# A decoder block on one core: the two halves of a two-bank PSUM tile used two blocks apart, a third pair of row buffers in the last phase, and late tiles opened two blocks sooner

## The chip, the core and the metric

The kernel runs on one core of a Trainium2 chip. The metric is the device time of one execution in microseconds (us). Three runs of the kernel before gave 1812.57, 1811.48 and 1809.37 us, so the median is 1811.48 us. A fourth run was profiled. All rows in this document are from profiles of that kind.

The engines have short names here. PE is the matrix engine, PEld its weight load. DVE is the vector engine, ACT the scalar engine, POOL the GpSimd engine and SP the engine that issues most transfers. SBUF is the on-chip working memory. PSUM is the accumulator memory that matmuls write to, in eight banks.

## The reference

One decoder layer runs over 512 tokens of width 1024, in fp32. It has two mixing branches (gated linear attention, and sliding-window attention with sinks), then a PEER layer: each token picks 128 of 16384 single-neuron experts and adds their outputs.

```python
h = rmsnorm(x); proj = h @ w_in                        # all head groups and gates
y_a = gla(...) @ w_branch_a;  y_b = swa(...) @ w_branch_b
x = x + (sigmoid(gate_a) * y_a + sigmoid(gate_b) * y_b) @ w_out
xn = rmsnorm(x)                                        # PEER from here
scores = per head, two halves of the query against 128 sub-keys each
idx, gate = top 16 of the 16 x 16 sums, softmax        # 8 heads x 16 = 128 experts a token
hid = gelu(einsum('lkd,ld->lk', expert_u[idx], xn))
x = x + einsum('lk,lkd->ld', gate * hid, expert_v[idx])
```

## The kernel before

The first 668 us hold the mixing branches and the scores. All that is changed lies behind, in the PEER layer, which the kernel computes in two ways at once.

**Dense part, 360 tokens.** All 16384 experts are taken in 128 blocks of 128. For block b, `h_step(b)` forms the first products (inputs times U rows, 24 matmuls of 360 columns into one PSUM bank, name `hp`), and ACT takes their gelu (line 1367) into an SBUF ring. Later `v_step(b)` multiplies the gelu by the gates (`w_a`, `w_b`) and adds it, against the V rows, into eight output banks. The blocks are done in three phases (`PHASES`, line 77): first products of blocks 0 to 91, second products of 0 to 91, first products of 92 to 111, second products of 92 to 111, first products of 112 to 127, second products of 112 to 127. The text calls these H0, V0, H1, V1, H2 and V2. Each 512 KB weight block is loaded by SP (`raw`), rounded by ACT (`whi`, line 149), and its rest is formed by DVE (`wlo`, line 159).

**Sparse part, 152 tokens.** The other tokens gather the U and V rows of their own experts. There are 154 slots of 1 MB (`gather`, line 1264). POOL issues a gather (line 1285). DVE does a product with the token (line 1300), ACT a gelu and a gate (lines 1258 and 1259), DVE an addition (line 1317). While H0 runs, a slot has a single buffer (`row`, two of them, in a pool `R`). From `late[0]` on, slots come in pairs (`rows`, tag `gbuf`, two buffers of 2 MB). `issue(k)` runs at the end of the addition of slot k-1 and requests all slots below a horizon of k + 2, and of k + 3 when late.

**What else lies in H0.** Scores become expert numbers and gates; the gates of the 360 dense tokens are built block by block with small matmuls (`gp`, line 1165), copied by ACT (`gbuild`, also tag `gbuf`) and written to memory (`gd`); one token group's gates go out by 128 scatters on POOL (line 1120). V0 reads them back as `gt` tiles (`g_load`, line 1382). The first two `g_load`s are issued on POOL at block `N0 - GL`; the tiles lie in a pool `Lt` that takes the memory of `R`, so the last early slot must be added up first (`while early[0]: step()`, at block `N0 - TAIL - 1`).

**Order.** Each engine runs its instructions in the order in which the program writes them. Where steps of the sparse part go between blocks is decided while the program is built: `pump` keeps running sums of the cost of PE, DVE, POOL and DMA work, and takes a step when the others are not ahead of PE.

**Banks of the first products.** In H0 blocks with b % 4 of 0 and 1 write the two halves of one two-bank tile (`hp2`, tag `S2`), blocks with b % 4 of 2 and 3 write single banks `M0` and `M1` (lines 1352 to 1357). The other banks are in use by `gp` and the transposes.

**The end.** The last two blocks of V2 are done column block by column block (c from 7 down to 0, line 1568). Each gets 6 matmuls, an addition on DVE (`yT`, line 1483), three transposes on PE (`yt`) two column blocks later, two additions into the output tile (`xr`, lines 1492 and 1493), and two steps of the sparse part. What is left of the sparse part comes behind (`flush`), then a last small product (`xo`) folds its sum in.

Of the kernel before, what the change touches and what calls it, by code (L numbers as in the profile page):

```python
# [47 lines left out]
NOO = 4  # L48
AHEAD = 3
LEAD = 23  # L50
TAIL = 3
SLACK = 3.0
DUTY = 0.97
LAND = 10.0
POOLQ = 9.0
GL = 4

HD = (3, 2, 2, 3, 2, 2, 2, 0, 0)
XG = 24
# [22 lines left out]
def tile_block(ctx, tc, xT, wst, smalls, wgk2, keysT, uT, vv, uv_rows, out):  # L82
# [1161 lines left out]
            yield  # L1244

    late, early, used, acc2 = [False], [0], [-1], []
    nxt, born, end = [], {}, [False]
    sel = XP.tile([128, XG], F32, name="sel")
    nc.gpsimd.tensor_tensor(sel, ident[:, 0:XG], ident[:, XG:2 * XG], OP.add)
    for r in range(2, XR):  # L1250
# [13 lines left out]
    def gather():  # L1264
# [7 lines left out]

        def issue(k):
            nonlocal grp, n
            while n < min(n_, k + (3 if late[0] else 2)):
                for i in range(min(2 if late[0] else 1, n_ - n)):
                    if late[0]:
                        if i == 0:
                            grp = Dn.tile([128, 2, 2 * D], F32, name="rows", tag="gbuf", bufs=2)
                        rows[n] = grp[:, i]  # L1280
                    else:
                        rows[n] = R.tile([128, 2 * D], F32, name="row", tag="er", bufs=2)
                        early[0] = n + 1
                    ix = use[slots[n][0]][3]
                    nc.gpsimd.indirect_dma_start(  # L1285
                        out=rows[n], out_offset=None, in_=uv_rows,
                        in_offset=bass.IndirectOffsetOnAxis(ap=ix[:, slots[n][1]:slots[n][1] + 1], axis=0))
                    n += 1
                    pool[0] += 1.5
                    born[n - 1] = max(pe[0], pool[0])  # L1290
                    xfer(2.54)
# [57 lines left out]

    def h_step(b, each=None):  # L1350
        w = get("U", b)
        if b < N0 and b % 4 < 2:
            if b % 2 == 0:
                two[0] = PS.tile([128, 2, 512], F32, name="hp2", tag="S2")
            bank = two[0][:, b % 2]
        else:
            bank = PS.tile([128, 512], F32, name="hp", tag=f"M{b % 2}")
        ps = proj(w, XN, n=TD, c0=TG, bank=bank, each=each)
        p = b // 2
        spill = NRP <= p < N0 // 2  # L1360
# [142 lines left out]
    for ph, (b0, b1) in enumerate(PHASES):  # L1503
# [38 lines left out]
        for c, tg in enumerate(BANKS):  # L1542
            accs[c] = big[:, c] if c < 2 else PS.tile([128, 512], F32, name="oa", tag=tg)
        last = b1 == NB
        for b in range(b0, b1 - 2 if last else b1):
            p = b // 2
            if not ph and b % 2 == 0 and p:
# [8 lines left out]
            v_step(b, b == b0, b == b1 - 1)  # L1556
            pump()
            if b == NB - 6:
                end[0] = True
                xr = P.tile([128, 4, D], F32, name="xr", tag="hhi")  # L1560
                nc.sync.dma_start(xr[0:TB, 1], x1s[XG:, 1])
                nc.sync.dma_start(xr[0:XG, 0], x1s[0:XG, 1])
# [95 lines left out]
```

## Time and profile before

| | us |
|---|---|
| median of three runs | 1811.48 |
| profiled execution, its own time | 1812.18 |
| its span, first to last instruction | 1810.4 |
| PE busy | 1727.5 (95%) |
| DVE busy | 1320.8 (73%) |
| ACT busy | 766.0 (42%) |
| POOL busy | 753.7 (42%) |
| PE idle for gelu in H0 (line 1367) | 16.9 |

The profiled execution lies 0.7 us above the median, and 1.8 us of it lie outside the span. PE is busy nearly all the time, so each microsecond in which PE stands still, or runs at the lower of its two clock levels (the profile gives the granted clock as a share of 2.4 GHz), is a candidate for a loss. A row of a timeline tells in brackets how long the engine stood idle before the instruction, and which instruction ended that. DMA share is the mean busy share of the core's 16 transfer engines.

### The profile page before, as it was taken

What the parts mean: (1) busy time and instruction counts of PE and PEld (TensorE: products, weight loads), DVE (VectorE), ACT (ScalarE), POOL (GpSimd) and SP (SyncE); (2) the same over time, 40 slices, a digit from 0 to 9 for tenths busy, and PEclk for the clock granted to TensorE, in tenths of its full rate; (3) what the DMA queues carried; (4) which work ended last, traced back from release to release, by engine and by line L of the source; (5) the groups of instructions that cost most, each with busy time, mean ns of one, the idle gap of its engine ahead of it and who ended that gap; (6) DMA issues with size and microseconds to landing.
All of it is one profiled execution on the core that took longest, in us unless ns stands there. A gap on an engine that the chain in (4) does not pass through costs nothing.

```text
span 1810.4 us, 26362 instructions
## 1 busy us (share of the span) xinstructions
PE 1727.5 (95%) x9828; PEld 1588.5 (88%) x9828; DVE 1320.8 (73%) x2547; ACT 766.0 (42%) x1350; POOL 753.7 (42%) x472
## 2 busy tenths in 40 slices
PE   7899999999997999999999999999999999999995
PEld 5676688987885889999999999999999999999993
DVE  7647714346246996987767745888988999898896
ACT  5445523335244234355455543444444444443441
POOL 3333444444544451677777671212222233233231
PEclk9999999999998999999999999999999999999996
DMA  4223542222243233589899898999999999999994
GB/s 159 77 70 94 149 133 81 70 82 73 91 143 132 77 108 135 137 254 258 263 275 276 246 296 314 392 400 400 396 401 405 379 379 394 355 393 350 402 346 175
DMA packets 164837, 432.68 MB, mean 239 GB/s; under 512 B 34789, under 2 KB 80229, under 8 KB 144613
## 3 DMA queue, kind: packets, MB, share of 16 engines
q1 hardware_dynamic: 118597, 254.69, 39.8%
q0 software_dynamic: 40928, 163.04, 25.5%
q10 hardware_dynamic: 5184, 13.27, 1.9%
q8 instruction: 77, 1.26, 0.3%
q14 instruction: 51, 0.42, 0.1%
HBM read 389.30 MB, written 41.62 MB: 238 GB/s over the span
## 4 chain that ended last, share of the span: by engine, by line
PE 78%; DVE 9%; DMA 5%; ACT 4%; issue 2%; POOL 1%; SPq 0%; POOLq 0%; DVEq 0%; ACTq 0%
PE hp L210 25%; PE oa L1419 19%; PE mm L210 17%; PE oacc L1419 6%; PE mm L227 4%; DMA rows<-in_uv_rows_dram,misc 4%; PE gp L1165 3%; PE sc L954 1%; DMA gt<-g 1%; DVE accy L1317 0%; DVE stt L434 0%; ACT hw L1367 0%; DMA xt<-in_xT_dram 0%; DVE stt L435 0%; DMA qb<-in_keysT_dram 0%
## 5 line engine op out<-in xcount | busy, mean ns | idle before, releaser
L149 ACT CAST whi<-raw 128x1024 fp32r<-128x1024 f32 x349 | 363.2, 1045 | 112.8 <-DMA raw<-in_vv_dram 22.5
L1285 POOL DMA_INDIRECT rows<-in_uv_rows_dram,misc x130 | 185.9, 1430 | 516.3 <-DVE accv L1317 405.6
L159 DVE TENSOR_TENSOR wlo<-raw,whi 128x1024 fp32r<-128x1024 f32 x250 | 306.0, 1224 | 103.2 <-issue 46.3
L210 PE MATMUL hp<-xh,whi 128*128 128x360 f32 x1024 | 344.3, 336 | 20.9 <-ACT hw L1367 13.4
L159 POOL TENSOR_TENSOR wlo<-raw,whi 128x1024 fp32r<-128x1024 f32 x99 | 245.0, 2478 | 242.8 <-ACT whi L149 230.0
L210 PE MATMUL hp<-xl,whi 128*128 128x360 f32 x1024 | 337.2, 329 | 0.0
L210 PE MATMUL hp<-xh,wlo 128*128 128x360 f32 x1024 | 336.3, 328 | 0.0
L1120 POOL DMA_INDIRECT g<-w,addr x128 | 229.9, 1796 | 90.0 <-issue 42.4
L1419 PE MATMUL oa<-wh,wlo 128*128 128x360 f32 x768 | 252.6, 329 | 1.0 <-DVE wlo L159 1.0
L1419 PE MATMUL oa<-wh,whi 128*128 128x360 f32 x768 | 252.9, 329 | 0.0
L1419 PE MATMUL oa<-wl,whi 128*128 128x360 f32 x768 | 252.1, 328 | 0.0
L210 PEld LDWEIGHTS hp<-xh,whi 128*128 128x128 f32 x1024 | 193.9, 189 | 28.0 <-ACT hw L1367 18.5
L210 PEld LDWEIGHTS hp<-xl,whi 128*128 128x128 f32 x1024 | 193.8, 189 | 0.0
L210 PEld LDWEIGHTS hp<-xh,wlo 128*128 128x128 f32 x1024 | 193.5, 189 | 0.0
L1419 PEld LDWEIGHTS oa<-wh,wlo 128*128 128x128 f32 x768 | 145.5, 189 | 1.3 <-DVE wlo L159 1.3
L1419 PEld LDWEIGHTS oa<-wl,whi 128*128 128x128 f32 x768 | 145.6, 190 | 0.0
L1419 PEld LDWEIGHTS oa<-wh,whi 128*128 128x128 f32 x768 | 145.6, 190 | 0.0
L1317 DVE SCALAR_TENSOR_TENSOR accv<-rows,misc,accv 128x1024 f32<-128x1024 f32 x104 | 133.5, 1284 | 11.8 <-ACT misc L1259 11.8
L1300 DVE SCALAR_TENSOR_TENSOR rows<-rows,xtok 128x1024 f32<-128x1024 f32 x104 | 127.1, 1222 | 5.5 <-DMA rows<-in_uv_rows_dram,misc 5.0
L1258 ACT ACTIVATE misc<-misc 128x1 f32<-128x1 f32 (+1 forms) x154 | 31.5, 204 | 221.7 <-DVE rows L1300 221.7
L210 PE MATMUL mm<-hhi,whi 128*128 128x512 f32 x264 | 107.1, 406 | 0.9 <-DVE gb L610 0.9
L210 PE MATMUL mm<-hhi,wlo 128*128 128x512 f32 x264 | 103.1, 391 | 0.0
(583 smaller groups left out, 3318.8 us busy)
## 6 DMA issues: line engine op xcount, KB each, us to landing
raw<-in_uT_dram SPq DMA_DIRECT2D x128, 512.0 KB, 5.5
raw<-in_vv_dram SPq DMA_DIRECT2D x128, 512.0 KB, 8.6
raw<-in_wst_dram SPq DMA_DIRECT2D x93, 512.0 KB, 3.5
gd<-gbuild SPq DMA_DIRECT2D x56, 256.0 KB, 6.0
gt<-gd SPq DMA_DIRECT2D x30, 464.0 KB, 10.6
hs<-hw ACTq DMA_DIRECT2D x36, 360.0 KB, 7.0
ring<-hs SPq DMA_DIRECT2D x36, 360.0 KB
g<-zero SPq DMA_DIRECT2D x16, 512.0 KB, 5.7
```

The source lines that it names most:

```text
L149: nc.scalar.copy(hi, self.raw[u])
L159: self.lo_eng(u).tensor_tensor(lo, r, hi.bitcast(F32), OP.subtract)
L210: nc.tensor.matmul(ps[:, :n], a[:, kb, :], b[:, kb, c0:c0 + n], start=(kb == 0 and i == 0), stop=(kb == KB - 1 and i == 2))
L227: nc.tensor.matmul(banks[t], a[:, kb, t * 128:(t + 1) * 128], b[:, k, :], start=(first and k == 0 and i == 0), stop=(last and k == kk - 1 ...
L954: nc.tensor.matmul(sc[:, t], qp[:, t * 128:(t + 1) * 128], ky[hp], start=True, stop=True)
L1120: i = nc.gpsimd.indirect_dma_start(out=g3, out_offset=bass.IndirectOffsetOnAxis(ap=addr[:, c:c + 1], axis=0), in_=w3[:, c:c + 1], in_offse ...
L1165: nc.tensor.matmul(p[:, k], o[:, 0, k], o[:, 1, k], start=True, stop=True)
L1258: nc.scalar.activation(h, h, AF.Gelu)
L1285: nc.gpsimd.indirect_dma_start(out=rows[n], out_offset=None, in_=uv_rows, in_offset=bass.IndirectOffsetOnAxis(ap=ix[:, slots[n][1]:slots[n ...
L1300: nc.vector.scalar_tensor_tensor(cur, cur, 1.0, xs_[kind][0:m, :], OP.mult, OP.mult, accum_out=hc)
L1317: nc.vector.scalar_tensor_tensor(a_, cur, h_[0:m, s_:s_ + 1], a_, OP.mult, OP.add)
L1419: nc.tensor.matmul(accs[c][:, 0:TD], v_[:, cs], a, start=(first and i == 0), stop=(last and i == 2))
```

## The change

Four edits. The halves of `hp2` now go to blocks with b % 4 of 0 and 2, and the blocks between them use `M0` and `M1` in turn. `GL` and `TAIL` each grow by 2, so that the first `g_load`s, the switch to pairs and the close of pool `R` come two blocks sooner (blocks 86, 83 and 86 in place of 88, 85 and 88), and the gate building is spread over 58 blocks in place of 60. In V2 a third pair buffer is used: the memory of the tag `hlo`, which held the low part of the inputs until the last first product. `end[0]` is set at the start of V2 in place of block 122, and while it holds, the horizon grows by 2; two products may run ahead of the additions, as they did from block 122 on before.

```diff
-TAIL = 3
+TAIL = 5
-GL = 4
+GL = 6
...
-            while n < min(n_, k + (3 if late[0] else 2)):
+            while n < min(n_, k + (3 if late[0] else 2) + 2 * end[0]):
...
-                            grp = Dn.tile([128, 2, 2 * D], F32, name="rows", tag="gbuf", bufs=2)
+                            pool_, tag, k_ = (P, "hlo", 1) if end[0] and en[0] % 3 == 0 else (Dn, "gbuf", 2)
+                            en[0] += end[0]
+                            grp = pool_.tile([128, 2, 2 * D], F32, name="rows", tag=tag, bufs=k_)
...
-        if b < N0 and b % 4 < 2:
-            if b % 2 == 0:
+        if b < N0 and b % 2 == 0:
+            if b % 4 == 0:
                 two[0] = PS.tile([128, 2, 512], F32, name="hp2", tag="S2")
-            bank = two[0][:, b % 2]
+            bank = two[0][:, b % 4 // 2]
         else:
-            bank = PS.tile([128, 512], F32, name="hp", tag=f"M{b % 2}")
+            bank = PS.tile([128, 512], F32, name="hp", tag=f"M{(b // 2 if b < N0 else b) % 2}")
...
         last = b1 == NB
+        end[0] = last
...
             if b == NB - 6:
-                end[0] = True
```

On PE, in H0, the first matmuls of blocks 8 to 13 stand like this before, with the semaphore that each waits for. `whi101` is the weight of block 8, and each next number is the next block; `hp2` is the two-bank tile, `hp` a single bank.

```order
L210 MATMUL hp2_5775<-xh_4270,whi101_5664 128x360 [waits Activation_49]
...
L210 MATMUL hp2_5775<-xh_4270,whi102_5695 128x360 [waits Activation_49]
...
L210 MATMUL hp_5843<-xh_4270,whi103_5728 128x360
...
L210 MATMUL hp_5880<-xh_4270,whi104_5771 128x360
...
L210 MATMUL hp2_5914<-xh_4270,whi105_5808 128x360 [waits Activation_49]
...
L210 MATMUL hp2_5914<-xh_4270,whi106_5839 128x360 [waits Activation_49]
```

The same six first matmuls on PE now:

```order
L210 MATMUL hp2_5775<-xh_4270,whi101_5664 128x360 [waits Activation_49]
...
L210 MATMUL hp_5812<-xh_4270,whi102_5696 128x360
...
L210 MATMUL hp2_5775<-xh_4270,whi103_5728 128x360 [waits Activation_49]
...
L210 MATMUL hp_5880<-xh_4270,whi104_5771 128x360
...
L210 MATMUL hp2_5914<-xh_4270,whi105_5808 128x360 [waits Activation_49]
...
L210 MATMUL hp_5953<-xh_4270,whi106_5840 128x360
```

The wait for ACT at the second half stood one block after the first half, and stands two blocks after it now; the wait of the next tile stood three blocks after the second half and stands two after it now.

On DVE, at the end, the work behind the `wlo` of the last weight block stands like this before. `accy` is an addition of the sparse part, `rows` with `misc` a product, `yT` and `xr` belong to the output columns.

```order
L159 TENSOR_TENSOR wlo_16062<-raw_15996,whi_16026 128x1024
L1317 SCALAR_TENSOR_TENSOR accy<-rows,misc,accy 120x1024
L1300 SCALAR_TENSOR_TENSOR rows,misc<-rows,xtk_14474 120x1024
L1483 TENSOR_TENSOR yT<-yT,oa 128x360
...
L1300 SCALAR_TENSOR_TENSOR rows,misc<-rows,xtk_14474 120x1024
L1483 TENSOR_TENSOR yT<-yT,oa 128x360
L1492 TENSOR_TENSOR xr<-xr,yt 104x128
L1493 TENSOR_TENSOR xr<-xr,yt 128x2x128
L1317 SCALAR_TENSOR_TENSOR accy<-rows,misc,accy 120x1024 x2
L1483 TENSOR_TENSOR yT<-yT,oacc 128x360
```

The same place on DVE now:

```order
L159 TENSOR_TENSOR wlo_16077<-raw_16010,whi_16041 128x1024
L1319 SCALAR_TENSOR_TENSOR accy<-rows,misc,accy 120x1024
L1302 SCALAR_TENSOR_TENSOR rows,misc<-rows,xtk_14370 120x1024
L1485 TENSOR_TENSOR yT<-yT,oa 128x360
...
L1302 SCALAR_TENSOR_TENSOR rows,misc<-rows,xtk_14370 120x1024
L1485 TENSOR_TENSOR yT<-yT,oa 128x360
L1494 TENSOR_TENSOR xr<-xr,yt 104x128
L1495 TENSOR_TENSOR xr<-xr,yt 128x2x128
L1319 SCALAR_TENSOR_TENSOR accy<-rows,misc,accy 120x1024 x2
L1485 TENSOR_TENSOR yT<-yT,oa 128x360
```

Behind that `wlo` stand 8 additions and 6 products before, and 6 additions and 4 products now. Before, the last two additions are followed by the seventh of the eight `yT`; now by the fifth. Counted from the start, two slots more are done at each of these points: 26 in place of 24 at the end of H0, 148 in place of 146 additions at the last `wlo`. Line numbers behind the edits are higher by 2.

## Rows read from the trace of the kernel before

**Rows 1.** Waits of PE, whole span: who, for whom, us, times, longest.

```profile
PE hp L210 <- ACT hw L1367: 13.4, 18, 1.8
...
PE hp L210 <- ACT ev L1473: 4.0, 1, 4.0
...
PE hp L210 <- ACT ring L1367: 3.5, 5, 1.2
```

**Rows 2.** The chain that ended last, merged: start, length, what, matmuls.

```profile
1065.50 16.21 PE hp L210 x96
1082.25 16.20 PE hp L210 x96
...
1481.04 59.70 PE hp L210 x360
```

**Rows 3.** Timeline of PE, in H0 and at the start of V0: start, length.

```profile
921.52 0.43 PE L210 MATMUL hp<-xh,whi 128*128 128x360 f32 x1 [1.80 <-ACT hw L1367]
...
922.65 0.50 PE L210 MATMUL hp<-xh,whi 128*128 128x360 f32 x1
922.95 0.50 PE L210 MATMUL hp<-xl,whi 128*128 128x360 f32 x1
...
925.65 0.48 PE L210 MATMUL hp<-xl,whi 128*128 128x360 f32 x1
...
1113.88 0.67 PE L1419 MATMUL oacc<-wh,whi 128*128 128x360 f32 x1 [2.70 <-ACT wh L1403]
...
1114.83 0.67 PE L1419 MATMUL oacc<-wl,whi 128*128 128x360 f32 x1 [0.27 <-DVE wl L1409]
...
1120.39 0.40 PE L1419 MATMUL oa<-wl,whi 128*128 128x360 f32 x1
```

**Rows 4.** Timeline of ACT, late in H0.

```profile
1093.38 1.05 ACT L149 CAST whi<-raw 128x1024 fp32r<-128x1024 f32 x1 [6.36 <-DMA hs<-hw]
1094.33 0.46 ACT L1367 ACTIVATE hw<-hp 128x360 f32<-128x360 f32 x1
```

**Rows 5.** Timeline of POOL, late in H0.

```profile
1094.84 1.64 POOL L1285 DMA_INDIRECT rows<-in_uv_rows_dram,misc  x1 [12.54 <-DMA raw<-in_uT_dram]
...
1101.36 0.59 POOL L1384 DMA_DIRECT2D gt<-gd  x1 [3.19 <-DVE accv L1317]
```

**Rows 6.** Timeline of DVE, from H0 into V0.

```profile
1099.40 1.28 DVE L1317 SCALAR_TENSOR_TENSOR accv<-row,misc,accv 128x1024 f32<-128x1024 f32 x1 [0.90 <-ACT misc L1259]
...
1112.52 0.44 DVE L1398 TENSOR_TENSOR wr<-ring,gt 128x272 f32<-128x272 f32 x1 [0.78 <-DMA gt<-g]
```

**Rows 7.** Stretches: length, busy PE, PEld, DVE, ACT, POOL, granted clock, DMA share, GB/s.

```profile
780.00:1110.00 330.00, 317.38 (x2025) 312.79 (x2024) 224.94 (x402) 159.98 (x234) 230.30 (x137) 0.99 0.92 276
960.00:990.00 30.00, 28.88 (x186) 28.28 (x185) 21.61 (x40) 15.43 (x24) 22.23 (x14) 1.00 0.97 277
1742.00:1752.00 10.00, 10.00 (x63) 10.00 (x61) 10.00 (x14) 5.45 (x9) 1.51 (x1) 1.00 1.02 396
```

**Rows 8.** Timeline of DVE at the end.

```profile
1767.61 1.22 DVE L159 TENSOR_TENSOR wlo<-raw,whi 128x1024 fp32r<-128x1024 f32 x1
1768.75 1.28 DVE L1317 SCALAR_TENSOR_TENSOR accy<-rows,misc,accy 120x1024 f32<-120x1024 f32 x1
```

**Rows 9.** DVE by line, 1768.7 to 1804: count, busy, mean ns, idle before.

```profile
L1317 DVE SCALAR_TENSOR_TENSOR accy<-rows,misc,accy 120x1024 f32<-120x1024 f32 x8 | 10.2, 1279 | 0.1
L1300 DVE SCALAR_TENSOR_TENSOR rows<-rows,xtk 120x1024 f32<-120x1024 f32 x6 | 7.4, 1226 | 6.9 <-DMA rows<-in_uv_rows_dram,misc 6.9
```

**Rows 10.** Timeline of SP, the last weight block's load.

```profile
1751.09 0.36 SPq L140 DMA_DIRECT2D raw<-in_vv_dram  x1
```

**Rows 11.** Timeline of ACT, the rounding of that block.

```profile
1765.28 1.05 ACT L149 CAST whi<-raw 128x1024 fp32r<-128x1024 f32 x1 [4.85 <-DMA raw<-in_vv_dram]
```

**Rows 12.** Transfers issued from 1712 to 1768: count, KB each, us to landing.

```profile
raw<-in_vv_dram SPq DMA_DIRECT2D x11, 512.0 KB, 7.1
...
rows<-in_uv_rows_dram,misc POOLq DMA_INDIRECT x10, 11.1
```

More of the change, by code (lines that the diff above doesn't have):

```diff
@@ L1246, in tile_block @@
     late, early, used, acc2 = [False], [0], [-1], []
-    nxt, born, end = [], {}, [False]
+    nxt, born, end, en = [], {}, [False], [0]
     sel = XP.tile([128, XG], F32, name="sel")
```

## The prediction

> **What bounds the kernel now.** I read the table of busy shares first: PE is busy 95% of the span, so the time is PE's work plus PE's gaps. The second view is the list of PE's waits [rows 1]. In H0 PE waits 23 times for a gelu: 13.4 us in 18 waits where the gelu goes into `hw`, 3.5 us in 5 where it goes into `ring`, together 16.9 us. At the end of V1 it waits 4.0 us for `ev`. The third view is PE's timeline, which shows what a gap costs beside its own length [rows 2, 3]. The fourth is the end on DVE and POOL [rows 8, 9]: behind the last `wlo`, at 1768.75, PE has only eight short column blocks left, and the end is set by DVE, which still has 8 additions and 6 products of the sparse part in its queue and stands idle 6.9 us for gathered rows that have not landed. The stretches tell what could take a gain back: from 780 to 1110 the transfer engines are busy 0.92 of the time [rows 7].
>
> **The halves of the two-bank tile.** Before, the second half's first matmul waits for the gelu of the first half, one block earlier and just finished. The reader sees this in the chain: two stretches of 96 matmuls, four blocks each, start at 1065.50 and 1082.25 [rows 2], 16.75 us apart. A stretch of 360 matmuls of H1, which has no such pairs, takes 59.70 us, 0.1658 us each, so 96 of them take 15.92. A pair therefore costs 0.83 us. Of that 0.54 is idle time (from the end of the first stretch, 1065.50 + 16.21, to 1082.25); the other 0.29 is the array filling again. For 23 pairs: 16.9 + 23 x 0.29 = 16.9 + 6.7 = 23.6 us. One wait, of 1.80 us at 921.52, is followed from 922.65 to 925.65 by matmuls 0.30 us apart [rows 3], which is the lower clock level of 1.2 GHz: 11 matmuls, each 0.134 us more than the 0.166 at 2.4 GHz, 1.5 us. Sum 25.1 us.
>
> With the new order one whole block lies between the gelu and the wait on either half, some 4.0 us (16.21 / 4). The largest gap that a late gelu made was 1.80 us, so 4 us of cover hide all 23. If the cover goes, a wait returns with 0.29 us on top. The cover is thinnest late in H0: ACT stood 6.36 us before a `whi` at 1093.38 and began a gelu only at 1094.33 [rows 4]. That gelu is of block 86 (88 ends at 1082.25 + 16.20 = 1098.45, so 86 ends near 1090.4), 3.9 us late, just inside the 4.0. I count no loss for it, and up to 2 us for the range.
>
> A rule of the Trainium skill speaks against any gain here. "Perfetto Trace Analysis", section "Matmuls" under "Optimizing Tensor Performance", says that independent groups should rotate through different PSUM banks so that the evacuation of one overlaps the matmuls of the next. The two halves are different banks already, so by that rule the wait would not be there, and the sum would be without the 25.1 us. The trace shows the wait, and the order of the instructions shows the semaphore that makes it, so the rows decide.
>
> **Two blocks sooner.** At the start of V0 the chain is: the addition of the last early slot (DVE, 1099.40) [rows 6], then the `g_load`s on POOL, behind it at 1101.36 [rows 5], landing in time for the second `wr` at 1112.52 [rows 6], then `wh` and PE at 1113.88 after 2.70 us idle, and 0.27 more [rows 3]. From 1114.83 to 1120.39 [rows 3] PE is at the lower clock level: 5.56 us at 0.30 us a matmul are some 18 of them, 18 x 0.134 = 2.4 us, and 0.3 for the slow first ones. Sum 5.7 us. Two blocks sooner is 8 us sooner against 2.97 us of lateness, so it goes, with 5 us to spare. What could eat the spare: POOL issues in order, and the second pair of late rows ahead of the `g_load`s waited 12.54 us, until 1094.84 [rows 5], for a buffer. That buffer is freed by the gate writes, which end two blocks sooner too, so I leave the margin as it is. If the margin went altogether, the 5.7 us would stay; nothing else hangs on it.
>
> The 58 gate groups are spread over 58 blocks in place of 60. PE's, DVE's and ACT's work for them is the same in sum. It costs nothing as long as transfers keep up; that is the next point. Two more slots are done in H0: two products and additions, 2 x (1.28 + 1.23) = 5.0 us of DVE, which is busy 225 of 330 us there, and 2 MB of transfers.
>
> **Transfers in H0.** At 0.92 of 330 us they need 303.6 us [rows 7], and two more slots at about 400 GB/s (the stretch at 1742) [rows 7] some 5.2 us: 309. If the part of the 25.1 us that lies in this stretch goes (four fifths of the pairs, 20 us), 310 us are left. That is a share of 1.00. A busy 30 us of that kind show 0.97. At 0.97 the 309 us would take 318.5, giving 8.5 us of the gain back; at 1.02, as in V2, nothing. Loads run some four blocks ahead, which buffers part of it. I take 3 us, and 0 to 8.5 for the range. V0, H1, V1 and H2 have the same work in the same order, two slots further on; I count nothing, and the wait of 4.0 us for `ev` stays.
>
> **The end.** With 148 in place of 146 additions at the last `wlo`, DVE loses 2 additions and 2 products behind it: 2 x (1.279 + 1.226) = 5.0 us of rows [rows 9]. Rows on DVE overlap a little (1.14 us from start to start for one of 1.22) [rows 8], so 4.7 us. The 6.9 us of idle time before products go if the rows have landed. The horizon requests the last pair at an addition that DVE reaches near the last `wlo`, some 13 us of DVE work ahead of its use, where gathers landed in 11.1 us (median) [rows 12]. So I take all of it: 11.6 us. PE's part of a column block, six matmuls (1.8 us even at 0.30) and three short transposes, is less than the 2.5 us of one product and one addition, so DVE goes on setting the pace. Bounds: 0, if the last `wlo` comes later by as much, and 13. The last `wlo` itself hangs on its weight block, issued at 1751.09 and landed for ACT at 1765.28, 14.2 us [rows 10, 11] against a median of 7.1 [rows 12]; the loads of the output tile go just ahead of it, as they do now, so I leave it.
>
> **Sum.** 25.1 + 5.7 + 11.6 - 3 = 39.4 us. The profiled execution took 1812.18 us: 1772.8. It lies 0.7 us above the median of the runs, so I predict 1772 us.
>
> **Rivals.**
> *Transfers bound H0.* If the share cannot rise above 0.92, H0 keeps its length from 780 on, and only the pairs ahead of 780 pay, one fifth, 5 us. Then 5 + 5.7 + 11.6 = 22 us, 1789 us. For it: the share is high and the gate writes are small pieces. Against it: PE never waited for a weight there, and neighbouring stretches reach 0.97.
>
> *The third pair starves V2.* One more pair in flight is 2 MB, 5.2 us at 400 GB/s, in a phase whose transfers are busy up to 1.02 [rows 7]. If it pushes the last weight block back by that, the end moves 5 us: 1777 us. The Trainium skill, "DMA: Bandwidth & Descriptors", section "Issuing engines are not separate DMA queues", says that transfers from SP, ACT and POOL run on the same 16 engines and interleave; by that rule POOL's pair takes time from SP's weight block. The trace agrees as far as it goes, with the 14.2 us above.
>
> *The wait moves and doesn't go.* If ACT and PE cannot work on the two halves at once for another reason than that semaphore, only the start of V0 and the end pay, 17.3 us: 1794 us. Against it: blocks on single banks show no gap while ACT empties others.
>
> *Slower than before: the gelu late by more than a block.* Each half is now reused with one block between, the tile as a whole too, where the next tile had two blocks of room. If ACT stands behind late weights as at 1093 [rows 4] throughout H0, there are 46 waits in place of 23. Each costs its excess x over 4.0 us plus 0.29. It turns the whole change slower once 46 (x + 0.29) passes the 42.4 us won, so from x = 0.63 us, a gelu 4.6 us late in every even block. At x = 1 it costs 59 us: 1811.5 - 42.4 + 59 = 1828 us. For it: one gelu was 3.9 us late, and transfers get denser. Against it: none of the 23 that PE waited for kept it over 1.80 us.
>
> **Chances.** Forecast 0.64 (its own range 1765 to 1782, from the 0 to 8.5 us of transfers, 2 us of ACT and 2 us at the end). Transfers bound H0: 0.16. Third pair: 0.11. Wait moves: 0.05. Slower: 0.03. One more 0.01 lies within 0.2% of before, about what a measurement of this kernel can tell from no change. Range 1763 to 1790 us: the lower end is the sum with no loss to transfers (1769), the wait for `ev` gone too (1765), and 2 us at the end. Faster 0.96, same 0.01, slower 0.03.
>
> **What would show it.** Right: no entry of PE waiting for L1367 in H0 over 1 us in sum; four pure blocks 16.0 us apart; no idle time and full clock at the start of V0; DVE without waits for rows behind the last `wlo`, and that `wlo` about 28 us sooner (25.1 + 5.7 - 3 = 27.8). Wrong: a DMA share of H0 that stays at 0.92 with new waits of PE or DVE for weights, or `whi` of the last block waiting longer than 4.85 us [rows 11]. The forecast fails if any of the three terms pays less than half.

## The result, and the profile after

The changed kernel takes 1790.27 us (median of 10 runs, 1781.76 to 1804.08) against 1811.81 us (10 runs, 1808.64 to 1817.55) beside it: ratio 0.9885, 95% interval 0.9859 to 0.9911. It is faster, by 21.5 us where 39.4 were forecast; 1790.27 lies just outside the range of 1763 to 1790. Two repeats (E4 and E12 below) gave ratios of 0.9839 (0.9800 to 0.9878) and 0.9893 (0.9865 to 0.9922).

The profiled run took 1782.82 us (span 1781.0), one of the two shortest of the ten. E12 was profiled in one of the longer ones, with a span of 1795.1. Both are needed, because what they differ by is part of what the forecast lacked. The lengths of the phases are taken from the start of each phase's first matmul in PE's timeline to the next one's (so that each wait ahead of a first matmul counts in the phase before it). What lies ahead of H0 (668.1, 668.6 and 667.5 us) is in no column:

| us | H0 with V0's first wait | V0 | H1 | V1 with the wait for `ev` | H2 | V2 and end | span |
|---|---|---|---|---|---|---|---|
| before | 445.8 | 367.1 | 79.7 | 84.0 | 66.0 | 99.7 | 1810.4 |
| after | 423.7 | 366.5 | 79.8 | 87.1 | 66.2 | 89.1 | 1781.0 |
| after, E12 | 432.0 | 368.4 | 80.5 | 84.4 | 72.1 | 90.3 | 1795.1 |

In the profile, H0 gives 22.1 us and the end 10.6; V1 takes 3.1 back. PE's waits of the changed kernel from 668 to 1130 us, the answer to [rows 1] (who, for whom, us in total, times, longest):

```profile
PE oacc L1421 <- ACT wh L1405: 2.2, 1, 2.2
PE hp L210 <- ACT hw L1369: 2.2, 3, 1.5
PE oacc L1421 <- DVE wl L1411: 0.5, 1, 0.5
```

The 23 waits for a gelu, 16.9 us, have become 3 waits and 2.2 us. V0's first wait, the first line, has hardly changed: 2.2 and 0.5 us where 2.70 and 0.27 stood [rows 3]. How it comes about is seen on POOL, DVE and PE in the order of time, the answer to [rows 3, 5, 6]. POOL, late in H0:

```profile
1064.45 1.54 POOL L1120 DMA_INDIRECT g<-w,addr  x1 [0.30 <-issue]
1066.30 1.33 POOL L1287 DMA_INDIRECT rows<-in_uv_rows_dram,misc  x1 [0.30 <-issue]
...
1070.82 0.94 POOL L1287 DMA_INDIRECT rows<-in_uv_rows_dram,misc  x1 [0.30 <-issue]
1076.14 0.59 POOL L1386 DMA_DIRECT2D gt<-gd  x1 [4.38 <-DVE accv L1319]
```

DVE, for the same tile and the last early slot:

```profile
1074.17 1.28 DVE L1319 SCALAR_TENSOR_TENSOR accv<-row,misc,accv 128x1024 f32<-128x1024 f32 x1 [0.60 <-ACT misc L1259]
...
1089.10 0.62 DVE L1400 TENSOR_TENSOR wr<-ring,gt 128x448 f32<-128x448 f32 x1 [5.32 <-DMA gt<-gd]
1090.92 0.44 DVE L1400 TENSOR_TENSOR wr<-ring,gt 128x272 f32<-128x272 f32 x1 [1.20 <-DMA gt<-g]
```

PE, V0's first matmul, and the stretch behind it in the view of stretches (busy PE, PEld, DVE, ACT, POOL, granted clock, DMA share, GB/s):

```profile
1092.29 0.43 PE L1421 MATMUL oacc<-wh,whi 128*128 128x360 f32 x1 [2.25 <-ACT wh L1405]
```

```profile
1040.00:1050.00 10.00, 10.00 (x62) 10.00 (x62) 8.20 (x8) 4.35 (x8) 8.48 (x6) 1.00 1.14 291
1092.20:1097.20 5.00, 4.41 (x17) 4.16 (x18) 4.93 (x7) 2.74 (x5) 0.00 (x0) 0.70 0.49 176
780.00:1110.00 330.00, 325.02 (x2089) 323.57 (x2088) 240.13 (x420) 165.06 (x252) 248.41 (x142) 0.99 0.97 298
```

POOL's scatters reach to 1066; then come the gathers of four rows, 4 MB; then POOL waits 4.38 us for the last early addition, and only then issues the `g_load`. Against V0's start that is 16.2 us ahead, where it was 12.5 before (1113.88 less 1101.36, [rows 3, 5]): 3.6 us of the 8 intended. The tile's transfers take longer from issue to landing (view of the tile `gt`, after and then before; least, median, most), 3.4 us in the median, and that eats what was left:

```profile
DMA to landing us min/median/max: 12.9/14.8/16.2
```

```profile
DMA to landing us min/median/max: 10.6/11.4/12.3
```

PE's granted clock is 0.70 in the mean of the five microseconds behind the wait, between its levels of 1.2 and 2.4 GHz. The last line answers to [rows 7]: from 780 to 1110 transfers are busy 0.97 of the time, with 18 us of V0 in it now (0.98 up to 1092).

E12 shows what a longer run of the same kernel has there. PE's waits for `hw` and `wh` (timeline of PE), and the same stretches:

```profile
1043.35 0.67 PE L210 MATMUL hp<-xh,whi 128*128 128x360 f32 x1 [4.39 <-ACT hw L1369]
...
1099.46 0.67 PE L1421 MATMUL oacc<-wh,whi 128*128 128x360 f32 x1 [6.17 <-ACT wh L1405]
```

```profile
1040.00:1050.00 10.00, 6.66 (x27) 6.66 (x28) 8.33 (x10) 3.90 (x9) 8.73 (x5) 0.66 0.83 206
1099.40:1104.40 5.00, 4.66 (x14) 4.28 (x15) 4.96 (x7) 2.74 (x5) 0.00 (x0) 0.50 0.45 150
```

A wait of 4.4 us for a gelu costs more than itself: in the ten microseconds from 1040 PE runs 27 matmuls where the other run has 62. The 35 missing ones are 5.8 us at 0.166; 3.35 of these are the wait's part up to 1043.35, the other 2.5 are the lower clock behind it (0.66 in the mean). With a first wait of 6.2 us, H0 is 8.3 us longer than in the other profile.

The end, the answer to [rows 8, 9 and 11]. DVE by line from 1751.8 to 1775 (count, busy, mean ns, idle before), and ACT's last `whi`:

```profile
L1319 DVE SCALAR_TENSOR_TENSOR accy<-rows,misc,accy 120x1024 f32<-120x1024 f32 x6 | 7.7, 1278 | 0.1
L1302 DVE SCALAR_TENSOR_TENSOR rows<-rows,xtk 120x1024 f32<-120x1024 f32 x4 | 4.9, 1215 | 0.0
```

```profile
1749.60 1.04 ACT L149 CAST whi<-raw 128x1024 fp32r<-128x1024 f32 x1 [7.21 <-DMA raw<-in_vv_dram]
```

Six additions and four products are left where there were eight and six, and the 6.9 us of idle time for rows are gone. ACT stands 7.21 us for the last weight block where it stood 4.85.

### The profile page after: what moved, and what is told of

It is laid out like the page before. It is cut to its first block, busy times and chain, and to the rows that moved or that the text cites. A ratio compares the mean times of both kernels' runs of the same rounds, so it can differ in the third digit from the quotient of the medians.

```text
span 1781.0 us, 26320 instructions
## 1 busy us (share of the span) xinstructions
PE 1721.4 (97%) x9828; PEld 1587.0 (89%) x9828; DVE 1317.8 (74%) x2547; ACT 763.2 (43%) x1350; POOL 761.1 (43%) x472
## 4 chain that ended last, share of the span: by engine, by line
PE 63%; DVE 11%; DMA 10%; POOL 7%; issue 5%; ACT 3%; SPq 1%; DVEq 0%; ACTq 0%; POOLq 0%
PE oa L1421 18%; PE mm L210 17%; PE hp L210 12%; PE oacc L1421 6%; POOL g L1120 6%; PE mm L227 4%; DMA rows<-in_uv_rows_dram,misc 4%; DMA raw<-in_vv_dram 2%; DMA g<-w,addr 1%; DMA row<-in_uv_rows_dram,misc 1%; PE gp L1165 1%; DVE wlo L159 1%; PE sc L954 1%; DVE accv L1319 1%; POOL row L1287 1%
## 5 line engine op out<-in xcount | busy, mean ns | idle before, releaser
L1287 POOL DMA_INDIRECT rows<-in_uv_rows_dram,misc x128 | 177.2, 1385 | 500.5 <-DVE accv L1319 413.3
L1120 POOL DMA_INDIRECT g<-w,addr x128 | 243.2, 1900 | 86.6 <-issue 40.6
L1319 DVE SCALAR_TENSOR_TENSOR accv<-rows,misc,accv 128x1024 f32<-128x1024 f32 x102 | 130.5, 1280 | 12.4 <-ACT misc L1259 12.4
L1166 ACT COPY gbuild<-gp 128x512 f32<-128x512 f32 x58 | 64.8, 1121 | 103.1 <-PE gp L1165 100.4
```

What stands on the lines that cost most here:

```text
L1120: i = nc.gpsimd.indirect_dma_start(out=g3, out_offset=bass.IndirectOffsetOnAxis(ap=addr[:, c:c + 1], axis=0), in_=w3[:, c:c + 1], in_offse ...
L1166: nc.scalar.copy(gbs[c].rearrange("p i t -> p t i")[:, q * 4:q * 4 + 4, :], p)
L1287: nc.gpsimd.indirect_dma_start(out=rows[n], out_offset=None, in_=uv_rows, in_offset=bass.IndirectOffsetOnAxis(ap=ix[:, slots[n][1]:slots[n ...
L1319: nc.vector.scalar_tensor_tensor(a_, cur, h_[0:m, s_:s_ + 1], a_, OP.mult, OP.add)
```

## The experiments

All were timed in 5 rounds beside the kernel before, whose medians on the four chips were 1815.5 (E1 to E4), 1813.9 (E5 to E8), 1814.2 (E9 to E12) and 1813.9 (E13 to E15). The columns are the phases of the table above; the phases come from one profiled run, the median from all. The time ahead of H0 (666.9 to 674.4 us in these profiles) is in no column.

| run | median us (lowest to highest) | ratio, 95% interval | H0 | V0 | H1 | V1 | H2 | V2, end |
|---|---|---|---|---|---|---|---|---|
| E1 halves | 1806.7 (1797 to 1817) | 0.9951 (0.9928 to 0.9975) | 441.3 | 366.2 | 79.7 | 87.7 | 65.9 | 101.2 |
| E2 sooner | 1817.6 (1811 to 1824) | 1.0017 (0.9999 to 1.0036) | 455.8 | 364.1 | 79.7 | 83.4 | 70.3 | 92.5 |
| E3 third pair | 1806.3 (1801 to 1814) | 0.9956 (0.9939 to 0.9974) | 443.5 | 364.8 | 79.9 | 88.3 | 66.2 | 95.4 |
| E4 changed kernel | 1784.0 (1780 to 1800) | 0.9839 (0.9800 to 0.9878) | 426.9 | 366.5 | 79.8 | 88.4 | 66.2 | 88.0 |
| E5 halves, sooner | 1789.5 (1786 to 1796) | 0.9874 (0.9847 to 0.9901) | 421.0 | 366.5 | 79.7 | 87.2 | 69.0 | 92.6 |
| E6 halves, third pair | 1801.6 (1801 to 1804) | 0.9938 (0.9918 to 0.9958) | 438.9 | 365.6 | 79.3 | 87.7 | 65.7 | 95.6 |
| E7 halves, few scatters | 1789.5 (1789 to 1792) | 0.9874 (0.9848 to 0.9900) | 424.1 | 366.0 | 79.7 | 84.7 | 65.4 | 99.2 |
| E8 GL 8, TAIL 7 | 1784.4 (1780 to 1798) | 0.9866 (0.9831 to 0.9901) | 426.2 | 364.7 | 79.7 | 83.1 | 68.0 | 89.9 |
| E9 gate load first | 1782.0 (1781 to 1789) | 0.9834 (0.9808 to 0.9861) | 423.6 | 364.1 | 79.7 | 84.5 | 66.8 | 93.1 |
| E10 step left out | 1784.3 (1777 to 1790) | 0.9827 (0.9800 to 0.9854) | 432.6 | 366.8 | 79.4 | 80.9 | 65.3 | 93.4 |
| E11 few scatters | 1785.0 (1782 to 1786) | 0.9840 (0.9816 to 0.9864) | 425.8 | 364.1 | 81.1 | 86.2 | 65.7 | 88.9 |
| E12 changed kernel | 1793.7 (1789 to 1803) | 0.9893 (0.9865 to 0.9922) | 432.0 | 368.4 | 80.5 | 84.4 | 72.1 | 90.3 |
| E13 E9 and E10 | 1780.9 (1780 to 1784) | 0.9813 (0.9800 to 0.9826) | 429.0 | 363.6 | 79.4 | 80.9 | 64.9 | 94.0 |
| E14 before, load first | 1820.5 (1817 to 1825) | 1.0038 (1.0025 to 1.0050) | 440.8 | 370.5 | 82.0 | 84.3 | 69.2 | 105.0 |
| E15 E6, load first | 1796.2 (1794 to 1807) | 0.9915 (0.9892 to 0.9938) | 419.7 | 368.8 | 81.3 | 85.7 | 65.9 | 98.4 |

**E1, E2, E3: one part each.** The edits are the lines of the change shown above: for E1 those of `h_step`, for E2 `TAIL` and `GL`, for E3 `issue` and `end[0]`.

> Only the halves of the two-bank tile two blocks apart. Theory (transfers bound H0): PE's waits for gelu in H0 fall from 16.9 us to under 3, but the DMA share from 780 to 1110 goes from 0.92 to about 0.97, weights and gate tiles land later, and the time varies more between executions; 14 to 20 us faster than before, with V0's first matmul waiting longer than 2.7 us. Rival (the third pair is what costs): nothing is lost here, 24 to 26 us faster, and executions agree as well as those of the kernel before.

> Only GL and TAIL larger by 2. Theory: two open slots are finished before the gate tiles are requested in place of one, some 3 us more on that chain, but with H0 otherwise at its old share of transfers the 8 us of lead cover it: V0 starts without idle time, 5 to 6 us, and two slots fewer behind the last weight block, 4 to 5 us; together 9 to 11 us faster. Rival (the lead is eaten by the open slots and by later landings whatever H0 does): the wait at V0 stays at 2 us or more and only the 4 to 5 us at the end pay.

> Only the third pair of row buffers and the early end flag. Theory: the 6.9 us of waits for rows behind the last weight block go, and up to 3 us are lost since that block lands later; 4 to 7 us faster. Rival (the third pair starves V2): the last weight block lands over 18 us after its issue and the time is within 2 us of before or slower.

Measured: 9 us faster, no faster (2 us slower, at the edge of what can be told), 9 us faster. Both theories missed E1 and E2, and E3 gained 2 us more than its theory's 4 to 7 (its profile has 4.3 of them at the end). In E3 the last weight block reached ACT 19.2 us after its issue, where it took 14.2 before: the rival's lateness came, but not its loss of time. For E1 and E2, H0 is where it went (E1's profiled run, 1811.6 us, lies 4.9 above its median). PE's waits there, in E1 and then in E2:

```profile
PE hp L210 <- DVE wlo L159: 6.9, 3, 5.2
PE oacc L1419 <- ACT wh L1403: 6.3, 1, 6.3
PE hp L210 <- ACT hw L1367: 4.9, 4, 1.6
```

```profile
PE hp L210 <- ACT hw L1367: 24.9, 18, 1.8
PE hp L210 <- ACT ring L1367: 3.6, 5, 1.3
```

In E1 the gelu waits fall from 16.9 to 4.9 us, but PE now waits 6.9 us for the low part of a weight and 6.3 us at V0's start. DVE makes that low part, and between 880 and 1110 us it waits like this, first in E1 and then in the kernel before, which has no such entry for rows:

```profile
DVE row L1300 <- DMA row<-in_uv_rows_dram,misc: 62.4, 12, 9.4
```

```profile
DVE wlo L159 <- issue: 26.7, 16, 2.9
DVE accv L1317 <- ACT misc L1259: 25.2, 13, 4.6
```

In E2 the waits are the 23 of before, but 28.5 us long. That what else ACT does in that order makes its gelus later is a reading, and no run tests it. V0's first wait was gone in E2, with H0 10 us longer, so I don't count it as a gain of the edit.

**E5, E6: two parts each.**

> Kernel before with the halves of the two-bank tile two blocks apart and the late tiles two blocks sooner, without the third pair. Theory (the two edits need each other in H0: the sooner late tiles alone make the gelus later by 11.6 us in sum, the halves hide just that, and the halves alone lose 62 us of DVE time to single-slot rows): H0 with V0's start 20 to 23 us shorter than before, the end as before, time 16 to 22 us under the kernel before. Rival (the surplus of the changed kernel over the sum of its parts comes from the third pair): H0 as in the halves alone, 6 to 9 us under the kernel before.

> Kernel before with the halves and the third pair, late tiles where they were. Theory: the two add, 9 + 9 = 18 us under the kernel before, with the 5.2 us wait of PE for a weight's low part in H0 still there. Rival (the third pair works only with a faster H0, or the reverse): 10 or less, or 22 or more under the kernel before.

E5 is 24.5 us faster where its parts alone give 7: the theory was right in sign and 2.5 us low. The sooner late tiles alone made the gelu waits longer, and with the halves moved those waits are gone; DVE's waits for rows come down to 33.9 us. E6 gave 12.4 where 18 was expected and 10 or less was the rival: neither. The third pair's gain is at the end (95.6 against 101.2 in E1), and most of the loss of E1 stays (PE still waits 4.4 us for a low part and 7.6 us at V0's start).

**E7, E11: POOL's queue.** The edit, on the halves alone and on the changed kernel, leaves out 120 of the 128 scatters:

```diff
-        nc.gpsimd.nop()
-        i = nc.gpsimd.indirect_dma_start(
...
+        if k == 0:
+            nc.gpsimd.nop()
+            i = nc.gpsimd.indirect_dma_start(
...
```

> The halves alone, with 8 of the 128 scatters of gate values on POOL left in (one per head), so the last 128 tokens' sparse gates are missing from the result. Theory (in the halves alone DVE waits for single-slot rows because POOL issues them late behind the scatters in its queue): DVE's 62 us of waits for rows between 880 and 1110 us fall below 15, PE's 5.2 us wait for a low part goes, V0 starts 8 us or more sooner than the 1109 us of the halves alone; time 8 to 14 us under it. Rival (the transfers are full there and the rows land late for that): the waits stay over 40 us, V0 starts within 3 us of 1109, and the time is within 4 us of the halves alone.

> The changed kernel with 8 of the 128 scatters of gate values on POOL left in (one per head), so the last 128 tokens' sparse gates are missing from the result. Theory (what is left of H0 over PE's own time, and the 24 us between the fastest and slowest run, come from POOL's queue): median 1776 to 1782, the runs within 5 us of each other. Rival (H0 is at PE's own time already and the spread comes from full transfers in V1 and V2): median within 3 us of the changed kernel's in the same call and a spread over 12 us.

E7 is 24.4 us under the kernel before on its chip, where the halves alone were 8.8 under theirs: 15.6 us (8 to 14 were expected). V0 starts at 1092.8 where E1 started at 1109.2, and DVE has no wait for a single-slot row left. The scatters use transfers too (the share from 880 to 1110 falls from 0.94 to 0.87), so the run takes both away. That the queue decides is read from E1 itself: from 960 to 1040, where DVE waited 27.9 us for rows, transfers were busy only 0.88. And POOL, which in the kernel before stood 23.2 us for DVE's additions ahead of its gathers (880 to 1075), has no such wait in E1, so its queue had no slack left (the stretch of E1, then the gathers before and in E1):

```profile
960.00:1040.00 80.00, 73.10 (x457) 72.20 (x456) 51.23 (x97) 36.70 (x54) 65.09 (x36) 0.96 0.88 243
```

```profile
L1285 POOL DMA_INDIRECT row<-in_uv_rows_dram,misc x15 | 21.8, 1456 | 25.7 <-DVE accv L1317 23.2 <-issue 1.8 <-DVE wlo L159 0.6
```

```profile
L1285 POOL DMA_INDIRECT row<-in_uv_rows_dram,misc x16 | 23.4, 1463 | 4.9 <-issue 3.4 <-DVE oh L1152 1.5
```

E11 fell between its two expectations: 8.7 us under E12 beside it, which the theory had, and runs within 4 us of each other, but a median of 1785.0, and its ratio is that of E4. So the shortest runs lose nothing to the scatters. Whether scatters make the longer runs long is not shown: without most of them the runs lay within 2.5 us (E7, 4 runs) and 4.0 (E11, 5 runs), and those of E1 within 20 (12 runs), but those of E6, which has all scatters and the H0 of E1, lay within 3.5 (6 runs) on E7's chip. E11 does settle whether transfers bound H0. They are busy 0.85 of it, where the changed kernel has 0.98, and H0 is no shorter, 425.8 us against 423.7:

```profile
780.00:1094.00 314.00, 309.49 (x1992) 308.87 (x1992) 223.73 (x402) 155.09 (x238) 72.53 (x38) 0.99 0.85 294
```

**E8: two blocks more** (`GL = 8`, `TAIL = 7`).

> The changed kernel with GL 8 and TAIL 7, two more blocks sooner. Theory (V0's first wait is left because POOL issues the gate tiles' load behind the last two single-slot rows, 16 us before V0 starts and 14 us in transfer; sooner by two blocks it has 32 us): no wait of PE for wh at V0's start and full clock there, H0 not longer, time 3 to 6 us under the changed kernel. Rival (as with the first two blocks, the rhythm of the sparse steps moves along and something else is late): V0's wait goes but H0 is longer by as much or more, time equal to the changed kernel or up to 10 us over it.

Neither: V0's first wait stays 2.2 us, and the time is that of E4, 1784. POOL issues the `g_load` without a wait for an addition, 21.4 us ahead of V0's start where it was 16.2, but still right behind four rows, and now the tile takes 21.0 us to land where it took 14.8:

```profile
1072.85 0.63 POOL L1386 DMA_DIRECT2D gt<-gd  x1
```

```profile
DMA to landing us min/median/max: 20.8/21.0/21.1
```

The first of the four rows is issued at 1066.30 in the changed kernel and at 1066.51 here, and DVE gets the tile at 1089.10 and 1091.30. So the moment at which POOL issues the load doesn't set when it lands, and what stands ahead of it does.

**E9, E14, E15: the gate tiles' load ahead of the rows.** No more rows are issued from the close of pool `R` until the load is out; the switch to pairs comes three blocks later with it, so it is not the order alone that changes:

```diff
         def issue(k):
+            if hold[0]:
+                return
...
-            if b == N0 - TAIL - 4:
-                late[0] = True
             if b == N0 - TAIL - 1:
+                late[0] = hold[0] = True
...
                 g_load(1, nc.gpsimd)
+                hold[0] = False
+                kick[0]()
```

> The changed kernel with the first two gate tiles' loads on POOL's queue ahead of the first four double rows instead of behind them (single-slot rows go on up to there). Theory (V0's first wait is left because four rows of 1 MB are in transfer ahead of the gate tiles, and POOL reaches the loads only behind its scatters): the gate tiles land 8 to 10 us sooner, PE's 2.2 us wait and the half clock at V0's start go, time 4 to 6 us under the changed kernel. Rival (the scatters in POOL's queue alone set it, or the rows' delay comes back as a late end): gate tiles land within 3 us of the changed kernel, or V2 is longer by as much; time within 2 us of it.

> The kernel before with nothing changed but the order on POOL's queue: gate tiles' loads ahead of the first four double rows. Theory (the rows ahead of the loads make V0's first wait in the kernel before too): PE's 2.7 us wait and the half clock behind it go, 4 to 7 us under the kernel before. Rival (there the late drain of the single-slot rows sets it, with 3 us of wait of POOL for the last sum in front of the loads): the wait stays over 1.5 us, time within 2 us of the kernel before.

> Halves and third pair, late tiles where they were in the kernel before, and the gate tiles' loads ahead of the rows on POOL. Theory (the sooner late tiles are needed in H0 only to keep DVE's steps off POOL's late rows, and V0's first wait is the order's): V0's 7.6 us wait goes, 5 to 9 us under the same without the new order (1801.6), so 1792 to 1797: still 10 or more over the version with sooner late tiles and new order (1782.0). Rival (the new order does all that the sooner late tiles do): 1780 to 1786.

E9 is 11.6 us under E12, the changed kernel on the same chip (4 to 6 were expected), and its runs stay within 8.4 us. Beside its own kernel before, its ratio is that of E4, so how much of the 11.6 us is the edit's stays open. The profile shows what became of the wait. On POOL and then DVE:

```profile
1078.10 0.62 POOL L1389 DMA_DIRECT2D gt<-gd  x1 [7.97 <-issue]
...
1080.72 1.55 POOL L1289 DMA_INDIRECT rows<-in_uv_rows_dram,misc  x1 [0.30 <-ACT hw L1372]
```

```profile
1085.65 0.97 DVE L1403 TENSOR_TENSOR wr<-ring,gt 128x448 f32<-128x448 f32 x2
```

The load is issued 2 us later than in the changed kernel, and yet the tile is used 7.6 us after its issue and without a wait, where the median landing was 14.8 (in E13, with the same order, the landing is on record: 6.0). The rows that went ahead of it made V0's first wait. What was in flight is seen in the four microseconds ahead of the load, here and in the changed kernel:

```profile
1074.00:1078.00 4.00, 4.00 (x26) 4.00 (x25) 3.40 (x5) 2.01 (x5) 0.00 (x0) 1.00 0.15 57
```

```profile
1072.00:1076.00 4.00, 4.00 (x26) 4.00 (x26) 3.40 (x5) 1.96 (x5) 0.00 (x0) 1.00 1.01 413
```

With the rows held back the transfer engines have nearly emptied (share 0.15) when the load comes; with the rows ahead they are full (1.01) and stay at 1.02 until the tile lands. E13, E14 and E15 have a gap of the same kind ahead of the load (0.13, 0.27 and 0.41). The five microseconds from V0's start have 33 matmuls where they had 17:

```profile
1091.80:1096.80 5.00, 5.00 (x33) 5.00 (x32) 5.00 (x8) 3.54 (x7) 0.00 (x0) 1.00 1.01 418
```

Part is given back: V2 and the end are 4.0 us longer than in the profile of the changed kernel. As much work is left behind the last `wlo` (six additions, four products), but that `wlo` comes 62.8 us behind V2's start where it came 58.8, and DVE stands 6.81 us for it, since its weight block is late. Whether that goes back to the gap in the transfers is not tested.

E14 missed on both accounts. V0's first wait is gone and H0 is 5.0 us shorter (2.7 of them are the wait), but the kernel is 6.5 us slower: V0 takes 3.4 us more (a new wait of PE for a `yT` copy, 3.1 us, at its end), H1 2.3, H2 3.2 and the end 5.3. At the end DVE has the same products left as in [rows 9] and waits longer for their rows:

```profile
L1303 DVE SCALAR_TENSOR_TENSOR rows<-rows,xtk 120x1024 f32<-120x1024 f32 x6 | 7.3, 1223 | 11.1 <-DMA rows<-in_uv_rows_dram,misc 11.1
```

So the order takes the wait away, and here the later phases took back more than it gave. In E9, with the third pair, DVE waits for no rows at the end. E15's time is as its theory had it, 5.4 us under E6 and 14 over E9, but not the place. In its profile, its fastest run, V0 starts at 1091.6 as in E9 (1091.8), PE has no wait listed in H0 and 0.95 us at V0's start. The 11.8 us between the two profiles lie behind V0's start: 4.7 in V0, 1.6 in H1, 1.2 in V1 and 5.3 at the end, less 0.8 in H2. So in H0 this edit does what the sooner late tiles do, and what they add shows later: the end has eight additions and six products left as before, and why V0 is longer is not settled.

**E10: V1's end.** The sparse step behind the last block of V0 and V1 is left out:

```diff
             v_step(b, b == b0, b == b1 - 1)
-            pump()
+            if last or b < b1 - 1:
+                pump()
```

> The changed kernel without the sparse step that stands behind the last block of V0 and of V1. Theory (PE's wait of 5.8 us at H2's start, 4.0 before, is ACT's copy of the sums standing behind the gelu of a row whose product DVE does late): the wait falls under 2 us, one or two slots move behind, time 1 to 4 us under the changed kernel. Rival (V1's weights are late for want of transfer, and PE only waits elsewhere): the wait goes but V1 with H2 stays as long within 1 us; time the same.

PE's waits of V1, in the changed kernel and then in E10:

```profile
PE hp L210 <- ACT ev L1475: 5.8, 1, 5.8
```

```profile
PE hp L210 <- ACT ev L1475: 1.8, 1, 1.8
```

V1 with H2 is 146.25 us where it was 153.3 after and 150.0 before. The wait fell under 2 us, as the theory had it: the copy to `ev` stood behind a gelu of the sparse part on ACT. One addition and two products more are left behind the last `wlo`, and the end is 4.3 us longer for it, so some 3 us are left in the profile. The 9.3 us of the medians (against E12; 1 to 4 were expected) are more than this explains: part is how the runs fell, and E10's profile itself had a first wait of 6.2 us in V0.

**E4, E12: the changed kernel again.**

> The changed kernel once more, for a second profile of it. Theory: a run nearer to its median than the first profile (1783 us) shows the difference in H0 and at the start of V0, with a DMA share near 1.0 there and PE waiting for weights or gate tiles. Rival: H0 and V0 are as in the first profile and the difference lies in V1 or V2, behind late weight blocks.

> The changed kernel once more, for the runs beside the other three and for a trace of one of its slower runs, if the profile falls on one. Theory: median 1784 to 1790, runs from 1780 to 1804; a slower run's extra time stands in H0 (POOL late, DVE without rows). Rival: it stands in V1, H2 and V2 (weights late).

E4's profile is 4.6 us over the one shown first: 3.2 in H0, 1.3 in V1 and 1.2 ahead of H0, less 1.1 at the end, so most of it is at the theory's place. Against the kernel before it gains 18.9 us in H0 and 11.7 at the end and loses 4.4 in V1. E12's 14.1 us over the profile shown first lie 8.3 in H0 with V0's first wait, 1.9 in V0, 3.2 in V1 and H2 together (H2 alone 5.9) and 1.2 at the end: mostly the theory's place, in part the rival's. H2 is longer by PE's wait at V2's start, ahead of which DVE stood 3.94 us for gathered rows; the first profile has 0.43 us there:

```profile
1704.82 0.67 PE L1421 MATMUL oacc<-wh,whi 128*128 128x360 f32 x1 [5.46 <-ACT wh L1405]
```

**E13: both repairs.**

> The changed kernel with the gate tiles' loads ahead of the rows on POOL and without the sparse step behind the last block of V0 and V1. Theory (the two losses are in different places and add): no wait at V0's start, under 2.5 us at H2's start, time 1775 to 1780, the runs within 10 us of each other. Rival (the slots held back come late at the end, V2 with its end is longer by what V1 gains): 1781 to 1786.

1780.9 us, ratio 0.9813 (0.9800 to 0.9826): the fastest median here, 33.0 us under the kernel before, and runs within 4.1 us of each other. It lies between the theory and the rival. V0's first wait is gone and the wait for `ev` is 1.7 us, but V2 and the end take 94.0, 4.9 more than in the changed kernel. Whether it beats E9, 1782.0 on another chip, is not settled, nor by how much it beats the changed kernel, whose three ratios run from 0.9839 to 0.9893.

## Why the prediction came out wrong, step by step

The median lies 18.3 us above the forecast of 1772. The step of the halves held; what failed is the margin of the second step, a wait that was counted as fixed, and one profile read as the median.

**The halves, 25.1 us, less 3 for transfers.** Without V0's first wait (2.70 us before, 2.25 after) H0 fell from 443.1 to 421.4 us: 21.7 us where 22.1 stood in the sum. In E12 it is 17.2. The size was right in this run, one of the two shortest, but two things that the step counted at nothing were in it. E2 showed that the sooner late tiles, with the gate groups spread over 58 blocks, are not free: alone they lengthen the gelu waits by 11.6 us. E1 showed that a faster PE alone outruns POOL's queue of scatters and single-slot gathers. Together (E5) they lose neither, which the sum by parts could not show.

**"Two blocks sooner is 8 us sooner against 2.97 us of lateness, so it goes, with 5 us to spare".** This step failed. It paid 0.4 us of wait and 0.6 in V0 where 5.7 were counted. The 5.7 as a price was not too high: 2.70 us of wait, and in the kernel before 41 matmuls in V0's first ten microseconds where the next ten hold 63, 22 x 0.166 = 3.6 us:

```profile
1113.80:1118.80 5.00, 4.64 (x14) 4.26 (x15) 4.94 (x7) 2.74 (x5) 0.00 (x0) 0.50 0.41 137
1118.80:1123.80 5.00, 5.00 (x27) 5.00 (x27) 4.24 (x6) 2.70 (x5) 0.00 (x0) 0.83 0.96 270
1123.80:1133.80 10.00, 10.00 (x63) 10.00 (x62) 8.31 (x12) 4.35 (x8) 2.77 (x2) 1.00 0.80 307
```

The margin was wrong: the step moved the load in the program, while POOL reached it only behind its scatters, four row gathers and the drain of the early slots, 3.6 us sooner and not 8. I took the 12.54 us of POOL [rows 5] as the thing that had to move. Once that was gone, all four rows (4 MB) went out in the 10 us ahead of the load, where two had, and it landed 3.4 us later after its issue. E8 showed that a still sooner load behind the same rows lands 21.0 us after its issue and saves nothing, and E9, E13, E14 and E15 that without the rows ahead the wait goes (0.95 us is left in E15). The text had said that the forecast fails if a term pays less than half.

**"I count nothing, and the wait of 4.0 us for `ev` stays".** V1 with its wait grew by 3.1 us in the profile. E10 showed that the wait was never fixed: it hangs on where a sparse step falls on ACT, which this change moved (E1 and E3, with one part each, have 8.3 us there).

**The end, 11.6 us.** Measured 10.6. The split was off: E2, which only has the two slots more, gives 7.2 (92.5 against 99.7), though H2 is 4.3 us longer there with a wait of 4.1 at V2's start, and E3, with the third pair, gives 4.3. The last `wlo` came 16.9 us sooner and not 28 (1750.68 against 1767.61), as the rest of the sum was short, and ACT's wait for its weight block passed the 4.85 us that the text had named as a warning.

**The median.** The sum was made on one profile and read as a median. The profile fell 10 us short of it (29.4 us won of 39.4): 4.7 at V0's first wait and clock, 3.1 in V1, 1.0 at the end, the rest in pieces of 0.5 and less. The other 7.5 us are the step from the profiled run to the median. The kernel before had runs within 9 us of each other, this one 22, and E12 has 8.3 us of its excess in H0, at late gelus and late gate tiles, and 5.9 in H2. That is where one longer run lost its time; which event starts a longer run is not settled.

**The rivals.** Transfers did not bound H0: the share rose from 0.92 to 0.97, PE's waits for gelus went, as forecast, and with the share down to 0.85 H0 was no shorter (E11). The 1789 us of that rival agree with the median, but by luck, for other reasons. The third pair did not starve V2: E3 is faster, and the end is shorter, though the last weight block took 16.5 us from its issue to ACT in the changed kernel and 19.2 in E3, where it took 14.2. The wait did not just move: 23 waits for gelus became 3. The gelu late by more than a block happened once in E12 and not in every block.

The Trainium skill, "DMA: Bandwidth & Descriptors", section "Issuing engines are not separate DMA queues", says that transfers run on the same 16 engines whoever issues them, and interleave. The traces agree as far as they go: the tile's time to landing fell from 14.8 us to 6.0 (E13) and at most 7.6 (E9) where the engines had nearly emptied ahead of the load (0.13 and 0.15), and not in E8, where they were full. Whether a load behind the rows is late because of its place in POOL's queue, or because any transfer is late on full engines, no run here tells apart.

## What to carry to other kernels

A load that is moved sooner in the program starts when its queue's engine reaches it, and lands behind what is in flight by then. So count all that this engine has to issue ahead of it, and the bytes in flight, before pricing the wait as gone. Parts of one change that share an in-order engine need not add: time them in pairs (here minus 9 and plus 2 alone made minus 24 together). Where many steps have little slack, the profile of one run is the good case, and the median belongs in the sum as a term of its own.

## What the runs showed of the hardware

One wait of PE of 4.4 us amid dense work took the granted clock to 0.66 over ten microseconds, 2.5 us on top of the wait, while 23 waits of 0.7 us in the mean had left it at 0.99 [rows 7], though the one of 1.80 us was followed by 3 us at the lower level [rows 3]. And a 1.4 MB load behind 4 MB of gathered rows landed 14.8 us after its issue, and 21.0 when it was issued sooner behind the same rows (E8), but 6.0 (E13) and 6.9 (E15) with the rows behind it, where the transfer engines' share had fallen to 0.13 and 0.41 in the four microseconds ahead of it.
